# A hybrid DiT step on one core: triangular-solve lanes moved in and out by VectorE's 32x32 transposes

## The chip, the cores and the metric

The kernel runs on one core of a Trainium2 chip. The metric is device time in microseconds (us) of one execution, the median of three runs. A profile of one further execution gives the trace. Engines are named as the profile names them: PE is TensorE's matrix products, PEld its weight loads, DVE is VectorE, ACT is ScalarE, POOL is GpSimd, SP issues the transfers.

## The reference

One layer of a hybrid backbone for two request groups, 2048 "sample" tokens and 128 "prompt" tokens, model width 1024. One input projection feeds four branches (gated DeltaNet, a gated spatial unit, multi-scale pooling, a Fourier mix); one output projection joins them. The change concerns the DeltaNet branch. In chunks of 64 tokens it inverts a unit lower-triangular 64x64 matrix per chunk, head and direction:

```python
A = jnp.where(strict, jnp.einsum("nbhid,nbhjd->nbhij", kb, kc) * decay_mat, 0.0)
Tinv = lax.linalg.triangular_solve(eye + A, jnp.broadcast_to(eye, A.shape), left_side=True, lower=True)
u = jnp.einsum("nbhij,nbhje->nbhie", Tinv, vc * bc[..., None])
w = jnp.einsum("nbhij,nbhjd->nbhid", Tinv, kb * jnp.exp(gcum)[..., None])
...
(S_fin, o) = lax.scan(step, S0, (q_dec, k_dec, u, w, qk, g_last))
```

## The kernel before

Tokens come in three groups (`phase_a(gi)`: 768, 768 and 640 tokens, that is 12, 12 and 10 chunks). A group takes its normalized tokens (`x_fin`, line 334: transposes of x on PE into PSUM, evicted by ACT, split into a high and a low part by DVE and POOL), projects them with `mm3` (line 250: three fp32r products for each k, by far the most PE work), convolves, and prepares the recurrence of two head pairs (`pair_pre`). `pair_pre` multiplies keys with keys (line 673) and queries with keys (line 703) on PE, scales them by decays that come back from DRAM as broadcast rows (`Pd`, `Po`, `Pf`), and writes the two diagonal 32x32 blocks of each 64x64 matrix into `Ld` and the off-diagonal block into `Lo`.

The diagonal blocks are inverted in "lanes": each (pair, direction, chunk) of a half-chunk is one partition, the 32x32 matrix lies in the free dimension, and `lanes_solve` runs 30 steps of two DVE products over all lanes (lines 741 and 743). To get there, `lanes_in` transposes `Ld` on PE (line 731, 32 for a group) into the PSUM tag `pa`, and ACT evicts with a sign change into `LL` (line 734). To get back, `lanes_out` makes 128 products with an identity for each group (line 767), half of them after a DVE copy that reorders `LL` (line 762), evicted by ACT (lines 771, 775) and DVE (line 772) into `XF` and `XE`. Then the off-diagonal block follows from two products (lines 783 and 784, then 792 and 793), and the result goes to DRAM (`rec_d`), from where the scan (line 1053 on) reads it.

PSUM has four tags here: `pj` with 3 buffers (projections), `pa` with 2, `pb` with 2, `pc` with 1. A tag's buffers are handed out in the order in which the program asks for them. The order of instructions on each engine is made by a scheduler at build time, in which `lanes()` of one group is spread over the next group's projections. At run time each engine goes through its list in order, so an instruction that waits holds all behind it on its engine.

## Time and profile before

| | |
|---|---|
| median of 3 runs | 1212.36 us (1209.45 to 1213.25) |
| profiled execution, its own time | 1211.1 us |
| its span, first to last instruction | 1209.3 us |
| PE busy | 1090.1 us, 90% |
| DVE busy | 815.1 us, 67% |
| ACT, POOL busy | 417.9 us, 432.6 us |
| mean granted PE clock | 0.952 |

The span is 1.8 us under the profiled execution's own time. A share of busy time is an average over the whole span; what limits a stretch is read from the windows of that stretch. The stretch from 225 to 662 us holds all work on lanes of the three groups.

### The profile page before, as it was taken

To read this page: it belongs to the slowest core of one execution; us is meant where nothing else is said; L and a number is where in the kernel's file an instruction comes from. 1 tells how busy PE (TensorE), PEld (TensorE's weight loads), DVE (VectorE), ACT (ScalarE), POOL (GpSimd) and SP (SyncE) were. 2 spreads that over 40 slices of the span, in tenths; PEclk is the share of its full clock that TensorE was granted. 3 is DMA by queue.
4 is the path that set the end of the run, shared out by engine and by line. 5 is a ranking of instruction groups with operands and counts; after the bars stand their busy time and mean duration, and the time that the engine had idled before them with its cause. 6 is when DMAs were issued, how large, how long until landed. Compare 5 with 4: busy or idle time off the path is not lost.

```text
span 1209.3 us, 29864 instructions
## 1 busy us (share of the span) xinstructions
PE 1090.1 (90%) x12211; PEld 986.3 (82%) x12211; DVE 815.1 (67%) x1864; ACT 417.9 (35%) x837; POOL 432.6 (36%) x429
## 2 busy tenths in 40 slices
PE   5888988998799698898979989898999889999997
PEld 2488977998779697875879888887899778999997
DVE  3666886799974699934884633784243488878665
ACT  2355667656565756123123111121111211111211
POOL 1347364726442237510231242232135343433212
PEclk9899998999879799898999999999999989999999
DMA  9879549943644564645264556589355645544331
GB/s 309 302 250 316 139 120 232 279 131 83 148 114 104 126 151 112 192 142 143 70 187 125 160 165 211 181 262 306 89 160 167 213 136 166 173 133 150 106 131 70
DMA packets 251391, 204.28 MB, mean 169 GB/s; under 512 B 109138, under 2 KB 218706, under 8 KB 250998
## 3 DMA queue, kind: packets, MB, share of 16 engines
q1 hardware_dynamic: 251254, 202.37, 56.7%
q8 instruction: 96, 1.57, 0.5%
q14 instruction: 41, 0.34, 0.1%
HBM read 138.86 MB, written 63.46 MB: 167 GB/s over the span
## 4 chain that ended last, share of the span: by engine, by line
PE 45%; DVE 17%; DMA 11%; issue 4%; ACT 3%; SPq 1%; POOL 1%; DVEq 0%; ACTq 0%; POOLq 0%
PE pj L250 34%; PE pa L1053 3%; DMA wst<-in_wt_dram 2%; DVE LL L743 2%; DVE ltmp L741 2%; DVE BIG L243 2%; DVE acc L842 1%; DMA X<-xd_d 1%; DMA ada<-in_ada_dram 1%; PE pb L1295 1%; DMA hr<-h_d 1%; DMA wos<-in_wo_dram 1%; DVE BIG L240 1%; DMA wst<-in_wv_dram 1%; PE pb L1393 1%
## 5 line engine op out<-in xcount | busy, mean ns | idle before, releaser
L250 PE MATMUL pj<-BIG 128*128 128x256 f32 (+4 forms) x3888 | 615.9, 313 | 16.7 <-ACT g L1222 4.0
L250 PEld LDWEIGHTS pj<-BIG 128*128 128x128 f32 x3888 | 560.9, 195 | 36.2 <-issue 10.8
L250 PE MATMUL pj<-BIG,yh 128*128 128x256 f32 x1088 | 197.5, 286 | 3.6 <-ACT BIG L1355 2.4
L243 POOL TENSOR_TENSOR BIG<-wst,BIG 128x512 fp32r<-128x512 f32 (+1 forms) x66 | 96.0, 1455 | 235.4 <-DVE BIG L240 137.3
L250 PEld LDWEIGHTS pj<-BIG,yh 128*128 128x128 f32 x1088 | 164.6, 190 | 7.0 <-ACT BIG L1355 2.6
L250 PE MATMUL pj<-BIG,yl 128*128 128x256 f32 x544 | 141.3, 284 | 0.0
L250 PEld LDWEIGHTS pj<-BIG,yl 128*128 128x128 f32 x544 | 98.7, 190 | 0.7
L240 DVE CAST BIG<-wst 128x512 fp32r<-128x512 f32 (+2 forms) x72 | 38.6, 540 | 74.8 <-DMA wst<-in_wt_dram 34.5
L1060 POOL TENSOR_TENSOR gS<-S,sc_s 128x256 f32<-128x256 f32 x32 | 20.9, 655 | 133.8 <-DVE S L1075 128.3
L842 DVE SCALAR_TENSOR_TENSOR acc<-raw,prm,acc 128x768 f32<-128x768 f32 (+1 forms) x72 | 64.2, 908 | 5.5 <-ACT acc L840 5.5
L1374 ACT ACTIVATE yh<-yt 128x768 fp32r<-128x768 f32 (+1 forms) x34 | 20.7, 629 | 128.9 <-issue 47.3
L1222 ACT ACTIVATE g<-pj 128x256 f32<-128x256 f32 (+1 forms) x64 | 23.3, 396 | 118.3 <-PE pj L250 111.8
L243 DVE TENSOR_TENSOR BIG<-wst,BIG 128x512 fp32r<-128x512 f32 (+1 forms) x66 | 53.4, 808 | 15.9 <-ACT BIG L242 13.8
L1413 POOL TENSOR_TENSOR z<-z,xs 128x1024 f32<-128x1024 f32 x16 | 41.8, 2612 | 57.1 <-DVE z L1405 52.0
L741 DVE TENSOR_TENSOR ltmp<-LL 128x60 f32<-128x60 f32 (+14 forms) x90 | 53.6, 595 | 4.5 <-ACT LL L734 3.1
L743 DVE TENSOR_TENSOR LL<-LL,ltmp 128x60 f32<-128x60 f32 (+14 forms) x90 | 55.3, 614 | 1.4
L242 ACT ACTIVATE BIG<-wst 128x512 fp32r<-128x512 f32 (+1 forms) x60 | 37.6, 632 | 35.3 <-DMA wst<-in_wt_dram 14.0
L354 POOL TENSOR_TENSOR BIG<-h,BIG 128x384 fp32r<-128x384 f32 (+2 forms) x28 | 26.7, 953 | 54.0 <-DVE BIG L353 37.4
L1075 DVE TENSOR_TENSOR S<-pa,gS 128x256 f32<-128x256 f32 x34 | 14.3, 420 | 42.1 <-PE pc L1053 35.0
L1375 DVE TENSOR_TENSOR yl<-yt,yh 128x768 fp32r<-128x768 f32 (+1 forms) x34 | 37.3, 1112 | 7.8 <-ACT yh L1374 7.8
L1405 DVE TENSOR_TENSOR z<-pj,gbc 128x256 f32<-128x256 f32 x68 | 26.0, 419 | 22.5 <-PE pj L250 22.2
L1071 ACT ACTIVATE xn<-pa 128x256 f32<-128x256 f32 x34 | 12.9, 381 | 80.8 <-PE pa L1053 73.2
(291 smaller groups left out, 1846.1 us busy)
## 6 DMA issues: line engine op xcount, KB each, us to landing
wst<-in_wt_dram SPq DMA_DIRECT2D x96, 256.0 KB, 3.5
R<-rec_d SPq DMA_DIRECT2D x136, 128.0 KB, 3.1
ada<-in_ada_dram SPq DMA_DIRECT2D x24, 512.0 KB, 5.3
C<-com_d SPq DMA_DIRECT2D x68, 128.0 KB, 3.1
xs<-xs_d SPq DMA_DIRECT2D x16, 512.0 KB
out_dram<-z SPq DMA_DIRECT2D x16, 512.0 KB, 3.1
x<-in_xs_dram SPq DMA_DIRECT2D x13, 512.0 KB
xs_d<-x SPq DMA_DIRECT2D x13, 512.0 KB, 6.1
```

The lines of the kernel that those rows point to most:

```text
L240: nc.vector.tensor_copy(hi[:, ks, a:a + w], st[:, :, :w])
L242: nc.scalar.activation(hi[:, ks, a:a + w], st[:, :, :w], AF.Copy)
L243: (nc.vector if k0 == 0 else nc.gpsimd).tensor_tensor(lo[:, ks, a:a + w], st[:, :, :w], hi[:, ks, a:a + w].bitcast(F32), op=ALU.subtract)
L250: nc.tensor.matmul(out, lh[a](k), rh[b](k), start=(k == first and i == 0), stop=(k == last and i == 2))
L354: (nc.gpsimd if f % 2 else nc.vector).tensor_tensor(hT[1][:, f, off:off + w], h, hi.bitcast(F32), op=ALU.subtract)
L741: nc.vector.tensor_tensor(tv, X[:, :, j, j + 1:32].unsqueeze(2).to_broadcast([128, 2, j, ni]), bc(X[:, :, 0:j, j], ni), op=ALU.mult)
L743: nc.vector.tensor_tensor(X[:, :, 0:j, j + 1:32], X[:, :, 0:j, j + 1:32], tv, op=ALU.add)
L842: nc.vector.scalar_tensor_tensor(o, raw[:, si + j:si + j + n], w[:, j:j + 1], o, op0=ALU.mult, op1=ALU.add)
L1053: nc.tensor.matmul(ps[o, q], lh(q)[hp], rh[hp, q])
L1375: nc.vector.tensor_tensor(yl[:, q], yt[:, q], yh[:, q].bitcast(F32), op=ALU.subtract)
L1405: nc.vector.tensor_tensor(z[:, ns], ps, gbc[:, cd, ns], op=ALU.mult)
L1413: nc.gpsimd.tensor_tensor(z, z, xs, op=ALU.add)
```

## The change

`Ld` is laid out as [128, direction, 32 lanes, 32], and `lanes_in` becomes one DVE transpose of 32x32 blocks for each direction, from `Ld` straight into `LL`; a lane's partition now stands for one diagonal block of one pair and chunk, and the direction lies in the free dimension, where before the partition stood for pair, direction and chunk, and the two blocks lay in the free dimension. The solve's instructions keep their number and sizes. The sign goes into the factor `nb`, the negative of `be`. `lanes_out` becomes four DVE transposes for each group: two out of `LL` into new tiles `XT0`, `XT1`, two in place on `LL`. The products for the off-diagonal block read these directly; ACT copies the diagonal blocks into `XF` (8 copies of 32 partitions for each group), whose empty halves POOL clears first (2 memsets for each group, `lanes_tile`). `LL` has one buffer where it had two. The key and query products of `pair_pre` take their PSUM from `pa` (2 buffers) where they took it from `pb` (2 buffers). `x_fin` in `phase_a` alternates between `pc` and `pa` where it used `pc` alone.

```diff
+        nc.vector.tensor_scalar(g.nb, g.be, -1.0, None, op0=ALU.mult)
...
-        Ldv = Ld[:, :g.nu].rearrange("p (r d c) j -> p r d c j", r=2, d=2)
+        Ldv = Ld[:, :, pair * nch:(pair + 1) * nch]
...
-            ps = pb()
+            ps = pa()
...
-                nc.vector.tensor_tensor(Ldv[:, pair, d, cs], Pd[:, d, cs], psk[h2][:, 0], op=ALU.mult)
-            nc.gpsimd.tensor_tensor(Ldv[:, pair, d], Ldv[:, pair, d], bc(g.be[:, pair, d], 32), op=ALU.mult)
+                nc.vector.tensor_tensor(Ldv[:, d, cs], Pd[:, d, cs], psk[h2][:, 0], op=ALU.mult)
+            nc.gpsimd.tensor_tensor(Ldv[:, d], Ldv[:, d], bc(g.nb[:, pair, d], 32), op=ALU.mult)
...
-    def lanes_in(Ld, LL, jbs=range(8)):
-        for jb in jbs:
-            ps = pa()
-            for j in range(4):
-                nc.tensor.transpose(ps[:64, j * 128:j * 128 + 128], Ld[:, :, jb * 4 + j], ident)
-            pv = ps[:64].rearrange("p (j c b i) -> p j c b i", c=2, b=2, i=32)
-            for c2, cp in enumerate(HALF):
-                nc.scalar.activation(LL[cp, jb * 4:jb * 4 + 4], pv[:, :, c2], AF.Copy, scale=-1.0)
+    def lanes_in(Ld, LL, d):
+        nc.vector.transpose(LL[:, d], Ld[:, d].rearrange("p l j -> p j l"))
 
     def lanes_solve(LL, js=(1, 31)):
-        X = LL.rearrange("p c b i -> p b c i")
+        X = LL
...
-        dg = LL.rearrange("p c b i -> p (c b i)")
-        for b in range(2):
-            nc.gpsimd.memset(dg[:, b * 32:b * 32 + 31 * 65 + 1:65], 1.0)
-
-    def lanes_out(g, LL, Lo):
-        nch, nu = g.nch, g.nu
-        XF = ln_.tile([128, 3072], F32, tag="L6", name="XF", bufs=1)
-        XA = XF.rearrange("p (r x) -> p r x", r=2)[:, :, :2 * nch * 64].rearrange("p r (d c j) -> p r d c j", d=2, j=64)
+        dg = LL.rearrange("p d c i -> p d (c i)")
+        for d in range(2):
+            nc.gpsimd.memset(dg[:, d, 0:31 * 33 + 1:33], 1.0)
+
+    def lanes_tile(g):
+        t = ln_.tile([128, 3072], F32, tag="L6", name="XF", bufs=1)
+        XA = t.rearrange("p (r x) -> p r x", r=2)[:, :, :2 * g.nch * 64].rearrange("p r (d c j) -> p r d c j", d=2, j=64)
+        for d in range(2):
+            nc.gpsimd.memset(XA[:, :, d, :, 32 * d:32 * d + 32], 0.0)
+        return XA
+
+    def lanes_out(g, LL, Lo, XA):
+        nch = g.nch
         XF = [XA[:, r] for r in range(2)]
-        XE = ln_.tile([128, 2, NCC, 32], F32, tag="XE", name="XE", bufs=1)[:, :, :nch]
-        for d in (1, 0):
-            for b8 in range(4):
-                ps = pa()
-                X2 = LL[:, b8 * 8:b8 * 8 + 8]
-                if d == 0:
-                    X2 = ln_.tile([128, 8, 2, 32], F32, tag="X2", name="X2", bufs=2)
-                    nc.vector.tensor_copy(X2, LL[:, :, :, b8 * 8:b8 * 8 + 8].rearrange("p c b i -> p i b c"))
-                X2 = X2.rearrange("p e b c -> p e (b c)")
-                for e in range(8):
-                    for c2, cp in enumerate(HALF):
-                        rows = slice(c2 * 64, c2 * 64 + nu)
-                        nc.tensor.matmul(ps[cp, e * nu:e * nu + nu], X2[rows, e], ident[rows, rows])
-                pv = ps[:, :8 * nu].rearrange("p (e r d c) -> p d r c e", e=8, r=2, d=2)
-                sl = slice(b8 * 8, b8 * 8 + 8)
-                s2 = slice(32 + b8 * 8, 40 + b8 * 8)
-                nc.scalar.activation(XA[:, :, d, :, sl], pv[:, d], AF.Copy, scale=K("ma"))
-                nc.vector.tensor_scalar(XA[:, :, d, :, s2], pv[:, d], K("mb"), None, op0=ALU.mult)
+        XD, XE = [None, None], [None, None]
+        for d, flip in ((1, 0), (0, 0), (0, 1), (1, 1)):
+            t = LL[:, d] if flip else ln_.tile([128, 32, 32], F32, tag=f"XT{d}", name="XT", bufs=1)
+            te = t.rearrange("p l e -> p e l")
+            nc.vector.transpose(te, te if flip else LL[:, d])
+            t = t[:, :2 * nch].rearrange("p (r c) e -> p r c e", r=2)
+            if flip == d:
+                XE[d] = t
+            else:
+                XD[d] = t
                 for c2 in range(2):
-                    q = slice(c2 * 64 + 32 * (1 - d), c2 * 64 + 32 * (1 - d) + 32)
-                    nc.scalar.activation(XE[q, :, :, sl], pv[q, 1 - d], AF.Copy)
-                yield 1
+                    for b in range(2):
+                        q = slice(c2 * 64 + b * 32, c2 * 64 + b * 32 + 32)
+                        nc.scalar.activation(XA[q, :, d, :, b * 32:b * 32 + 32], t[q], AF.Copy)
+            yield 1
         for r in range(2):
             ps = pa()
             for c in range(nch):
                 for h2 in range(2):
                     a = slice(h2 * 64, h2 * 64 + 32)
                     b = slice(h2 * 64 + 32, h2 * 64 + 64)
...
-                    nc.tensor.matmul(ps[a, c * 32:c * 32 + 32], Lo[b, r, c], XF[r][b, 0, c, 32:64])
-                    nc.tensor.matmul(ps[b, c * 32:c * 32 + 32], Lo[a, r, c], XF[r][a, 1, c, 0:32])
+                    nc.tensor.matmul(ps[a, c * 32:c * 32 + 32], Lo[b, r, c], XD[0][b, r, c])
+                    nc.tensor.matmul(ps[b, c * 32:c * 32 + 32], Lo[a, r, c], XD[1][a, r, c])
...
-                    nc.tensor.matmul(ps[a, c * 32:c * 32 + 32], XE[a, r, c], M1[a, c])
-                    nc.tensor.matmul(ps[b, c * 32:c * 32 + 32], XE[b, r, c], M1[b, c])
+                    nc.tensor.matmul(ps[a, c * 32:c * 32 + 32], XE[0][a, r, c], M1[a, c])
+                    nc.tensor.matmul(ps[b, c * 32:c * 32 + 32], XE[1][b, r, c], M1[b, c])
...
-            x_fin(preps.pop(0))
+            x_fin(preps.pop(0), range(KC), (pc, pa))
...
-                    LL = ln_.tile([128, 32, 2, 32], F32, tag="LL", name="LL", bufs=2)
-
                     def lanes():
-                        for jb in range(8):
-                            lanes_in(Ld, LL, (jb,))
+                        LL = ln_.tile([128, 2, 32, 32], F32, tag="LL", name="LL", bufs=1)
+                        for d in range(2):
+                            lanes_in(Ld, LL, d)
                             yield 1
                         lin.pop()
+                        XA = lanes_tile(g)
                         for a, b in zip(SPL, SPL[1:]):
                             lanes_solve(LL, (a, b))
                             yield 1
-                        yield from lanes_out(g, LL, Lo)
+                        yield from lanes_out(g, LL, Lo, XA)
```

On PE, before: the products out of lanes of the second group (line 767), which stand behind the key and query products of the third group's second pair (lines 673 and 703; 1295 is the gate row's product). The off-diagonal products follow them.

```order
L673 MATMUL pb<-sl 32x64 x40
L250 MATMUL pj<-BIG 128x320 x31
L703 MATMUL pb<-sl 64x64 x20
L250 MATMUL pj<-BIG 128x320 x103
L767 MATMUL pa<-cm,LL 64x48 x32
L250 MATMUL pj<-BIG 128x320 x21
L767 MATMUL pa<-cm,LL 64x48 x32
L250 MATMUL pj<-BIG 128x320 x21
L767 MATMUL pa<-cm,X_5251 64x48 x16
L767 MATMUL pa<-cm,X_5274 64x48 x16
L250 MATMUL pj<-BIG 128x320 x11
L1295 MATMUL pb<-ada_6755,csil 2x256 x4
```

After, at the same place: the end of the off-diagonal products of the second group (785 and 786, the former 792 and 793), and behind them the third group's key products (674) and query products (704), now in `pa`.

```order
L785 MATMUL pa<-M_5073,XT 32x32
L786 MATMUL pa<-M_5073,LL 32x32
L674 MATMUL pa<-sl 32x64 x20
L1288 MATMUL pb<-ada_6128,csil 2x256 x4
L250 MATMUL pj<-BIG 128x320 x11
L1288 MATMUL pb<-ada_6134,csil 2x256 x2
L674 MATMUL pa<-sl 32x64 x20
L704 MATMUL pa<-sl 64x64 x10
L1288 MATMUL pb<-ada_6134,csil 2x256 x2
L250 MATMUL pj<-BIG 128x256 x16
L704 MATMUL pa<-sl 64x64 x10
```

The products out of lanes are gone, and the third group's key and query products have moved from ahead of the second group's off-diagonal products to behind them.

On DVE, before: the end of the second group's solve, the reordering copies (762) and the evictions (772), with weight casts (240, 243) between.

```order
L743 TENSOR_TENSOR LL<-LL,ltmp 128x2x29x2
L741 TENSOR_TENSOR ltmp<-LL 128x60
L743 TENSOR_TENSOR LL<-LL,ltmp 128x2x30
L762 COPY X_5251<-LL 128x512
L762 COPY X_5274<-LL 128x512
L772 TENSOR_SCALAR XF<-pa,cm 128x2x12x8 x4
L240 CAST BIG<-wst 128x4x136
L243 TENSOR_TENSOR BIG<-wst,BIG 128x4x136
L762 COPY X_5297<-LL 128x512
L772 TENSOR_SCALAR XF<-pa,cm 128x2x12x8
L762 COPY X_5320<-LL 128x512
L772 TENSOR_SCALAR XF<-pa,cm 128x2x12x8
```

After, at the same place: the end of the solve, the four transposes (759), and the products that follow (779 and 791 are the former 786 and 798; 684 is the former 683).

```order
L736 TENSOR_TENSOR ltmp<-LL 128x60
L738 TENSOR_TENSOR LL<-LL,ltmp 128x2x30
L759 STREAM_TRANSPOSE XT<-LL 128x32x32 x2
L759 STREAM_TRANSPOSE LL<-LL 128x32x32 x2
L779 TENSOR_TENSOR M_4967<-pa,m1s_1830 128x384
L791 COPY XF<-pa 32x12x32 x2
L779 TENSOR_TENSOR M_5073<-pa,m1s_1830 128x384
L240 CAST BIG<-wst 128x4x136
L243 TENSOR_TENSOR BIG<-wst,BIG 128x4x136
L791 COPY XF<-pa 32x12x32
L684 TENSOR_TENSOR Ld<-Pd,pa 128x160 x2
```

The four transposes follow the solve with nothing between, and nothing on DVE waits for PE there until line 779.

On PE, before: the second group's x transposes for the third group (342), all in `pc`, among the key products (673) and query products (703) in `pb`.

```order
L342 MATMUL pc<-cm,x 128x128 x3
L250 MATMUL pj<-BIG 128x384
L250 MATMUL pj<-BIG 128x392 x15
L342 MATMUL pc<-cm,x 128x128 x3
L673 MATMUL pb<-sl 32x64 x48
L250 MATMUL pj<-BIG 128x272 x19
L342 MATMUL pc<-cm,x 128x128
L250 MATMUL pj<-BIG 128x272 x7
L703 MATMUL pb<-sl 64x64 x11
L342 MATMUL pc<-cm,x 128x128
```

After: the same x transposes, in `pa` and `pc`, directly behind the query products (704), which are in `pa` too.

```order
L704 MATMUL pa<-sl 64x64 x24
L250 MATMUL pj<-BIG 128x392 x17
L342 MATMUL pa<-cm,x 128x128 x3
L643 MATMUL pb<-cm,sl 128x128 x6
L342 MATMUL pa<-cm,x 128x128 x6
L342 MATMUL pc<-cm,x 128x128 x3
L250 MATMUL pj<-BIG 128x272 x3
L342 MATMUL pa<-cm,x 128x128 x3
L250 MATMUL pj<-BIG 128x272 x24
L342 MATMUL pc<-cm,x 128x128 x3
L342 MATMUL pa<-cm,x 128x128
```

The x transposes and the key and query products now share the two buffers of `pa`, and the transposes have moved behind the query products.

## Rows read from the trace of the kernel before

**Rows 1.** The page: PE's and DVE's busy time, and PE's granted clock.

```profile
PE 1090.1 (90%) x12211; PEld 986.3 (82%) x12211; DVE 815.1 (67%) x1864; ACT 417.9 (35%) x837; POOL 432.6 (36%) x429
PEclk9899998999879799898999999999999989999999
```

**Rows 2.** The page: the chain that ended last, share of the span by engine.

```profile
PE 45%; DVE 17%; DMA 11%; issue 4%; ACT 3%; SPq 1%; POOL 1%; DVEq 0%; ACTq 0%; POOLq 0%
```

**Rows 3.** Windows: start:end, us, busy PE, PEld, DVE, ACT, POOL, clock, DMA, GB/s.

```profile
225.00:260.00 35.00, 33.35 (x240) 31.05 (x239) 32.35 (x70) 18.46 (x42) 16.50 (x16) 1.00 0.70 213
260.00:295.00 35.00, 31.43 (x190) 30.30 (x189) 34.72 (x51) 22.42 (x36) 14.82 (x17) 1.00 0.42 107
295.00:330.00 35.00, 28.57 (x296) 26.85 (x297) 34.79 (x64) 17.47 (x30) 20.92 (x20) 0.85 0.52 123
330.00:350.00 20.00, 18.06 (x219) 15.03 (x218) 15.23 (x55) 13.48 (x33) 5.45 (x11) 0.78 0.67 162
445.00:505.00 60.00, 55.54 (x481) 53.40 (x482) 59.54 (x112) 26.40 (x45) 35.95 (x48) 0.97 0.60 150
505.00:530.00 25.00, 21.03 (x264) 19.23 (x263) 11.98 (x24) 8.01 (x22) 3.59 (x4) 0.80 0.45 149
225.00:662.00 437.00, 390.74 (x4548) 351.95 (x4546) 337.25 (x686) 198.99 (x422) 154.69 (x176) 0.93 0.51 137
```

**Rows 4.** Windows of line L731 alone (transposes into lanes), PE.

```profile
225.00:260.00 35.00, 6.41 (x32) 4.01 (x32) 1.00 0.70 213
395.00:445.00 50.00, 5.36 (x32) 3.53 (x32) 0.86 0.53 123
550.00:580.00 30.00, 4.78 (x32) 3.47 (x32) 0.95 0.41 106
```

**Rows 5.** Windows of line L767 alone (products out of lanes), PE.

```profile
330.00:350.00 20.00, 9.31 (x146) 7.96 (x147) 0.78 0.67 162
350.00:395.00 45.00, 6.39 (x116) 5.29 (x114) 0.91 0.38 92
505.00:550.00 45.00, 9.86 (x256) 9.36 (x256) 0.84 0.56 176
610.00:645.00 35.00, 8.64 (x256) 7.93 (x256) 0.95 0.51 160
```

**Rows 6.** Groups by line, PE: busy, mean ns, idle before and its releaser.

```profile
L767 PE MATMUL pa<-cm,LL 48*64 48x48 f32 (+1 forms) x384 | 18.4, 253 | 6.1 <-DVE LL L743 4.0 <-ACT XE L775 2.1
L767 PE MATMUL pa<-cm,X 48*64 48x48 f32 (+1 forms) x384 | 15.8, 237 | 0.3 <-ACT XE L775 0.3
```

**Rows 7.** Groups by line, DVE: the lane copies and evictions; the weight casts.

```profile
L762 DVE COPY X<-LL 128x512 f32<-128x512 f32 x12 | 9.6, 824 | 0.1
L772 DVE TENSOR_SCALAR XF<-pa,cm 128x192 f32<-128x192 f32 (+1 forms) x24 | 9.7, 403 | 17.9 <-ACT XF L771 17.7
L240 DVE CAST BIG<-wst 128x512 fp32r<-128x512 f32 (+2 forms) x72 | 38.6, 540 | 74.8 <-DMA wst<-in_wt_dram 34.5 <-PE pj L250 32.6 <-DMA wst<-in_wv_dram 3.0
```

**Rows 8.** Groups by line, ACT: evictions into and out of lanes.

```profile
L734 ACT ACTIVATE LL<-pa 64x256 f32<-64x256 f32 x48 | 18.0, 375 | 25.8 <-PE pa L731 25.4
L771 ACT ACTIVATE XF<-pa,cm 128x192 f32<-128x192 f32 (+1 forms) x24 | 9.9, 411 | 27.5 <-PE pa L767 27.2
L775 ACT ACTIVATE XE<-pa 32x192 f32<-32x192 f32 (+1 forms) x48 | 15.0, 312 | 16.3 <-DVE XF L772 15.9
```

**Rows 9.** Timeline: DVE's solve beside a POOL product; start, us, what.

```profile
505.27 0.39 DVE L741 TENSOR_TENSOR ltmp<-LL 128x216 f32<-128x216 f32 x1
505.32 3.38 POOL L1244 TENSOR_TENSOR rw<-rw,g 128x640 f32<-128x640 f32 x2 [0.37 <-DMA rw<-raw_d]
505.69 1.61 DVE L743 TENSOR_TENSOR LL<-LL,ltmp 128x216 f32<-128x216 f32 x1
```

**Rows 10.** Waits: who for whom, total us, times, longest.

```profile
POOL Pf L692 <- DMA Pf<-pf_d: 16.3, 3, 10.6
```

**Rows 11.** Groups by form, POOL: the clearing of Ld.

```profile
L964 POOL MEMSET Ld<- 128x768 f32 x1 | 0.7, 742 | 3.6 <-PE pa L731 3.6
```

More of the change, by code (lines that the diff above doesn't have):

```diff
@@ L915, in phase_a @@
         if gi:
-            x_fin(preps.pop(0))
+            x_fin(preps.pop(0), range(KC), (pc, pa))
         if gi == 1:
-            x_fin(preps.pop(0))
+            x_fin(preps.pop(0), range(KC), (pc, pa))
         elif gi == 2:
-            x_fin(preps.pop(0))
-            x_fin(x_prep([(16, 128)], 512, None))
+            x_fin(preps.pop(0), range(KC), (pc, pa))
+            x_fin(x_prep([(16, 128)], 512, None), range(KC), (pc, pa))
         lg = sm_.tile([128, 6, 16], F32, tag="lg", name="lg", bufs=1)
```

8 lines of the change are left out of this document (4 added, 4 removed).

## Prediction

> **What bounds the kernel now.** I read the page first. PE is busy for 1090.1 of 1209.3 us, 90%, and its granted clock is near full in most slices [rows 1]; the chain that ended last runs through PE for 45% and through DVE for 17% [rows 2]. So the kernel is bound by PE, with stretches in which DVE is the later engine. An average doesn't say where, so I cut the stretch that holds the lanes, 225 to 662 us, into windows [rows 3]. Over the whole stretch PE is busy for 390.74 of 437 us and DVE for 337.25. The reader is to see that DVE has no room in three windows, 260 to 295, 295 to 330 and 445 to 505 us (34.72, 34.79 and 59.54 us busy of 35, 35 and 60): there PE time taken out comes back as PE idle time. In 330 to 350 and 505 to 530 us it is the other way round: DVE has 5 and 13 us of room, and PE works at a granted clock of 0.78 and 0.80. Then I read the lines that go, by window and by group.
>
> **What the change removes.** On PE, the 96 transposes of line 731 take 6.41, 5.36 and 4.78 us in the three groups [rows 4], together 16.55. The products of line 767 take 9.31 + 6.39 us in the first group, 9.86 in the second and 8.64 in the third [rows 5], together 34.20. That is 50.75 us of PE time; nothing of it moves to PE elsewhere. PE also stood idle for 6.1 + 0.3 = 6.4 us just before line 767 [rows 6]. On DVE, the copies of line 762 and the evictions of line 772 go, 9.6 + 9.7 = 19.3 us [rows 7]. On ACT, 18.0 + 9.9 + 15.0 = 42.9 us go [rows 8].
>
> **What it adds.** Six 32x32 transposes for each group on DVE, each of 128x1024, 18 in all. No row shows one. The nearest from below is the cast of line 240, 0.540 us for 512 elements, so 1.08 for 1024; from above the reordering copy of line 762, 0.824 us for 512 as a mean, so 1.65 [rows 7]. I take 1.3, in the lower half, because the transpose reads one tensor that it streams once, as the cast does, while the copy's mean holds some that were held up. 18 x 1.3 = 23.4 us (19.4 to 29.7), 4 us more than DVE loses. DVE's total thus hardly changes, and where it is full it stays full.
>
> On ACT come 24 copies of 32x768 (32x640 in the third group). Line 775 moves 192 elements in 0.312 us [rows 8]; four times that, 1.25 us, bounds one from above and 0.312 from below, so 7 to 30 us against the 42.9 removed. ACT is busy for 199 of 437 us in the stretch [rows 3], and the copies feed only the transfer to DRAM and not the next product, so I count them at nothing; without that cover the last group's copies would delay the scan's first load by 8 x 1.25 = 10 us at most. POOL gets six memsets of 128x768; one such took 0.742 us [rows 11], 4.5 us in all, issued ahead of the solve that separates them from their reader, and the solve covers them. The three multiplications for `nb` touch 48 elements for each partition, below the 216-element product's 0.39 us [rows 9]: 1.2 us at most, hidden while DVE has room.
>
> The Trainium skill, page "VectorE: DVE Perf Modes", section "The three transpose paths", speaks against my 1.3 us. It gives 311 ns for a 128x128 transpose on VectorE in a 16-bit type, and 390 ns on TensorE. Scaled to 1024 columns, an estimate from that page, a transpose here would take 2.49 us, 18 would take 44.8, and the sum below would end at 1183 in place of 1172. No row here shows a DVE transpose.
>
> **Where it lies on the path.** In the first group line 731's 6.41 us stand at the head of the full DVE stretch (DVE 32.35 of 35, then 34.72 of 35), so I count them at nothing. The other 44.34 us stand where PE limits or is the one waited for. The 6.4 us of idle time before line 767 go with it, but a new wait takes its place: the off-diagonal products now need three of the four outgoing transposes behind the solve, 3 x 1.3 = 3.9 us for each group, 11.7 in all (9.7 to 14.9), if no projection stands ahead of them on PE. Queued behind the waiting product are the next projections of line 250, so this counts in full. The incoming pair of transposes (2.6 us) replaces a passage through PE and ACT whose waits were 25.4 us at ACT [rows 8]; I count no gain for that.
>
> The sum: 50.75 - 6.41 + 6.4 - 11.7 = 39.0 us. From the profiled execution's 1211.1 us this gives 1172.1. The median of the runs is 1212.36, 1.3 us above that execution, so I forecast 1173.
>
> The tags. The key and query products exchange two buffers of `pb` for two of `pa`; in `pb` they shared with the transposes of tokens, in `pa` with the off-diagonal products and half the x transposes. In the third group the key products move behind the second group's off-diagonal products, since `pa` is handed out in order; the evictions that they then wait for are one for each engine (about 0.5 us), and projections stand between the two halves. I count the exchange at nothing; its price if that is wrong is the last rival. `LL` with one buffer makes the next group's incoming transposes wait for the last products that read it; in the trace of before the next group's line 731 runs from 395 us on, when the first group's work out of lanes (ended by 395) is over [rows 4, 5], so the wait is there already.
>
> **The rivals.**
>
> *DVE becomes the bound (1193 us).* All that is taken from PE before 505 us only brings PE sooner to where the second group's solve ends, and the full window 445 to 505 us decides that end. For it: 59.54 of 60 us busy; against it: between 330 and 350 us DVE has room and PE is busy for 18.06 of 20, so DVE's work there can come sooner with PE's. Lost are 6.41 + 9.31 + 6.39 + 5.36 = 27.47 us; 23.3 + 6.4 - 11.7 = 18.0 remain.
>
> *More comes back (1146 to 1154 us).* All 50.75 and the 6.4 count and projections cover the new waits: 1211.1 - 57.2 = 1154. If the idle time that goes also lifts the granted clock in 295 to 350 and 505 to 530 us (0.85, 0.78, 0.80), up to 0.15 x 28.57 + 0.22 x 18.06 + 0.20 x 21.03 = 12.5 us more are there; with two thirds of it 1146.
>
> *The transposes are slow (1183 to 1210 us).* At twice the upper bound, 3.3 us, the five of each group that stand on the chain (two in, three out) cost 49.5 us and the gain is gone. From about 2.5 us they cost 10 us more than I count. Against it: the copy of line 762 reorders with a stride too, and even its mean gives 1.65.
>
> A rule beside it concerns POOL. In the trace a solve product of 216 elements took 1.61 us while POOL multiplied, its neighbour of the same size 0.39 [rows 9]. The Trainium skill, page "SBUF — State Buffer", section "Who interferes with whom", says that a DVE instruction with two SBUF inputs is blocked by a POOL instruction that reads SBUF, and one with a single input outside the two-port modes is not; the trace agrees with the first half. By it a transpose would be spared such holds.
>
> *A wait on `pa` takes the place (slower, 1236 us).* The x transposes stand directly behind the query products in `pa`, and a query product's buffer is free only when `Pf` has come back from DRAM and passed POOL, ACT and DVE. POOL waited for that load for up to 10.6 us [rows 10]. If PE stands still that long behind each of the six pairs, 64 us are lost: 1173 + 63 = 1236. It decides from 39 / 6 = 6.5 us for each pair. Against it: `pb` was bound to the same chain before, and the key products now stand earlier in the first group.
>
> **How the numbers follow.** Chances: the forecast 0.52, DVE as the bound 0.18, more comes back 0.14, slow transposes 0.07 (0.03 of it without a measurable change), the wait on `pa` 0.09. The forecast's own range is 1158 to 1186 (the transposes' bounds and the order's changes). The range 1147 to 1200 takes in the second and most of the third and fourth case, and leaves out some 0.17. Within 0.3%, 3.6 us, a measurement of this kernel can't tell a change from none. Faster: 0.52 + 0.18 + 0.14 + 0.04 = 0.88; same 0.03; slower 0.09.
>
> **What would show it.** Right: PE busy near 1039 us, no PE row of lines 731 and 767, a transpose of 128x1024 near 1.3 us, DVE's busy time near 820 us, PE waiting for a transpose before the off-diagonal products for about 4 us a group, and the stretch of lanes shorter by some 39 us with the rest as long as before. Wrong: a transpose over 2.5 us; PE's idle time in the stretch (46 us before) grown by over 20 us and put down to DVE's solve; or PE waiting in `pa` behind `Pf`.

## The result, and the profile after

The changed kernel takes 1199.39 us (median of 4 runs, 1196.99 to 1202.51); the kernel before, beside it, 1212.32 us. The ratio is 0.9896 (95% interval 0.9861 to 0.9931): 12.6 us faster, where 39 were forecast. The time lies at the upper end of the range, and 26 us above the forecast. The profiled execution took 1200.81 us, its span is 1199.0 us.

The page of the changed kernel answers to [rows 1, 2]: PE's busy time, its granted clock by slice, and the chain that ended last.

```profile
PE 1058.8 (88%) x11347; PEld 958.3 (80%) x11347; DVE 842.1 (70%) x1849; ACT 401.8 (34%) x746; POOL 437.4 (36%) x435
PEclk9899896999879989989789999899999889999999
PE 40%; DVE 24%; DMA 11%; issue 5%; ACT 4%; SPq 2%; POOL 1%; DVEq 0%; ACTq 0%; POOLq 0%
```

PE is busy 31.3 us less, not 50.75; DVE 27 us more, not 4; DVE's share of the chain rose from 17% to 24%. Of DVE's 27 us, 16.0 are the transposes less what they replace (35.3, the sum of their groups below, less 19.3). Another 14.6 lie behind 840 us, at a subtraction that the change doesn't touch (line 1375 before, 1368 after):

```profile
L1375 DVE TENSOR_TENSOR yl<-yt,yh 128x768 fp32r<-128x768 f32 (+1 forms) x34 | 37.3, 1112 | 7.8 <-ACT yh L1374 7.8
L1368 DVE TENSOR_TENSOR yl<-yt,yh 128x768 fp32r<-128x768 f32 (+1 forms) x34 | 51.9, 1543 | 12.5 <-ACT yh L1367 12.5
```

The windows answer to [rows 3]:

```profile
225.00:260.00 35.00, 29.19 (x205) 27.48 (x205) 33.72 (x71) 14.91 (x28) 17.38 (x18) 1.00 0.61 197
260.00:295.00 35.00, 32.09 (x273) 30.26 (x272) 32.67 (x56) 22.06 (x34) 14.45 (x12) 1.00 0.45 111
295.00:330.00 35.00, 27.25 (x196) 24.56 (x195) 34.79 (x63) 21.67 (x34) 20.77 (x23) 0.87 0.53 125
330.00:350.00 20.00, 13.08 (x101) 12.09 (x100) 20.00 (x34) 14.55 (x24) 10.52 (x11) 0.84 0.67 183
505.00:530.00 25.00, 17.09 (x470) 10.19 (x468) 12.81 (x17) 9.53 (x15) 0.00 (x0) 0.80 0.50 145
225.00:662.00 437.00, 371.80 (x3909) 332.56 (x3908) 367.20 (x701) 185.86 (x340) 165.25 (x185) 0.92 0.54 147
```

In 330 to 350 us, where PE was busy for 18.06 of 20 us and DVE had room, DVE is now full and PE busy for 13.08. The clock in 505 to 530 us is still 0.80, though the products out of lanes that ran there are gone; the second group's off-diagonal products, among others, run there now (from 511 us on). The groups by line show the new instructions (busy, mean ns of one, idle before):

```profile
L729 DVE STREAM_TRANSPOSE LL<-Ld 128x1024 f32<-128x1024 f32 x6 | 12.2, 2042 | 0.0
L759 DVE STREAM_TRANSPOSE LL<-LL 128x1024 f32<-128x1024 f32 x6 | 12.0, 2052 | 0.0
L759 DVE STREAM_TRANSPOSE XT<-LL 128x1024 f32<-128x1024 f32 x6 | 11.1, 1927 | 0.2
```

A transpose takes 1.93 to 2.05 us as a mean of its group, 35.3 us in all. And the waits of PE in 225 to 662 us (who for whom, total us, times, longest):

```profile
PE pb L643 <- DVE qeps L594: 5.8, 3, 2.8
PE pa L776 <- DVE LL L759: 4.9, 1, 4.9
...
PE pb L588 <- DVE S L847: 4.1, 2, 3.6
PE pc L342 <- DVE x L331: 3.4, 2, 2.7
```

PE waited once for an outgoing transpose (line 776, first group, 4.9 us). Its other waits for DVE in these rows are at lines of which the change touches only the PSUM tag of line 342. Summed by the engine waited for, over 220 to 660 us:

| PE waited for, us | before | changed | e1 | e16 | e21 |
|---|---|---|---|---|---|
| DVE | 18.1 | 36.6 | 54.8 | 51.5 | 33.4 |
| ACT | 22.1 | 17.6 | 15.0 | 19.3 | 17.9 |

The idle time of the stretch grew by 19 us, and PE's waits for DVE grew by 18.5 (e1, e16 and e21 are experiments, described below).

**An account of the span.** For each window of 20 us I multiplied PE's busy time by the granted clock. The sum is PE's work at full clock; the rest of the busy time is lost to the lower clock; span less busy time is idle. The three make up the span. They are those of one profiled execution for each kernel, which lies up to 11 us from the median of its runs (e3: 1206.4 against 1195.3). With the steps of the clock as the trace has them, in place of windows, work is 1040.2 us before and 995.2 in the changed kernel; a term is good to some 4 us. The profiled execution of e18 took 3271.67 us, so e18 has no account.

| kernel | time, us | ratio to before (95%) | work | clock loss | idle |
|---|---|---|---|---|---|
| before | 1212.3 | | 1041.3 | 48.8 | 119.2 |
| changed | 1199.4 | 0.9896 (0.9861 to 0.9931) | 997.9 | 60.9 | 140.2 |
| e1 lanes only | 1221.6 | 1.0092 (1.0077 to 1.0107) | 994.0 | 71.5 | 154.8 |
| e2 tags only | 1237.9 | 1.0242 (1.0190 to 1.0293) | 1041.3 | 67.0 | 125.5 |
| e3 x in pc | 1195.3 | 0.9886 (0.9852 to 0.9920) | 1003.2 | 60.0 | 141.3 |
| e4 keys in pb | 1202.0 | 0.9925 (0.9897 to 0.9953) | 997.7 | 56.0 | 141.6 |
| e6 out, one eighth | 1184.9 | 0.9759 (0.9706 to 0.9811) | 1019.4 | 48.3 | 114.0 |
| e14 in, one quarter | 1229.8 | 1.0134 (1.0088 to 1.0181) | 1033.5 | 74.7 | 121.0 |
| e7 transposes twice | 1214.9 | 1.0005 (0.9973 to 1.0038) | 999.4 | 60.9 | 147.8 |
| e15 no flips | 1188.5 | 0.9799 (0.9746 to 0.9853) | 998.7 | 50.4 | 134.8 |
| e11 contiguous | 1203.0 | 0.9936 (0.9899 to 0.9973) | 1001.9 | 58.4 | 138.7 |
| e8 half of casts on ACT | 1195.1 | 0.9853 (0.9798 to 0.9909) | 996.7 | 49.8 | 144.6 |
| e12 = e11 and e8 | 1202.3 | 0.9889 (0.9855 to 0.9923) | 1000.2 | 51.6 | 140.0 |
| e18 all casts on ACT | 1198.5 | 0.9866 (0.9780 to 0.9953) | | | |
| e9 before, casts as e8 | 1219.7 | 1.0049 (1.0013 to 1.0086) | 1033.9 | 55.7 | 125.1 |
| e16 one step | 1220.5 | 1.0075 (1.0038 to 1.0111) | 996.6 | 58.4 | 163.0 |
| e17 tags swapped | 1196.0 | 0.9862 (0.9785 to 0.9939) | 997.4 | 60.8 | 143.3 |
| e19 more steps | 1202.1 | 0.9877 (0.9827 to 0.9928) | 1004.5 | 55.7 | 141.8 |
| e21 lanes only, later | 1208.0 | 0.9955 (0.9923 to 0.9987) | 997.9 | 68.1 | 136.2 |

The changed kernel has 43.4 us less work, 12.1 more clock loss and 21.0 more idle time: -10.3 us of span. Of the idle time 19.0 us (46.2 to 65.2) came in 220 to 660 us. The work column moves little among kernels with the same PE instructions (994 to 1005; before and e2 1041.3, but e9 1033.9), so a difference of 7 us in it says nothing; the other two columns decide. Differences in us below are ratios times 1212.3.

### The profile page after: what moved, and what is told of

Read it like the earlier page. It is cut to its first block, busy times and chain, and to the rows that moved or that the text cites. A ratio compares the mean times of both kernels' runs of the same rounds, so it can differ in the third digit from the quotient of the medians.

```text
span 1199.0 us, 28014 instructions
## 1 busy us (share of the span) xinstructions
PE 1058.8 (88%) x11347; PEld 958.3 (80%) x11347; DVE 842.1 (70%) x1849; ACT 401.8 (34%) x746; POOL 437.4 (36%) x435
## 4 chain that ended last, share of the span: by engine, by line
PE 40%; DVE 24%; DMA 11%; issue 5%; ACT 4%; SPq 2%; POOL 1%; DVEq 0%; ACTq 0%; POOLq 0%
PE pj L250 31%; DMA wst<-in_wt_dram 4%; PE pa L1046 3%; DVE acc L835 2%; DVE ltmp L736 2%; DVE LL L738 2%; DVE BIG L243 2%; DMA R<-rec_d 1%; DVE yl L1368 1%; PE pb L1288 1%; DVE BIG L1210 1%; POOL BIG L243 1%; DVE LL L729 1%; DVE BIG L240 1%; DMA ada<-in_ada_dram 1%
## 5 line engine op out<-in xcount | busy, mean ns | idle before, releaser
L250 PE MATMUL pj<-BIG 128*128 128x256 f32 (+4 forms) x3888 | 622.6, 317 | 23.9 <-ACT raw L816 6.0
L250 PEld LDWEIGHTS pj<-BIG 128*128 128x128 f32 x3888 | 571.9, 199 | 45.8 <-issue 11.2
L243 POOL TENSOR_TENSOR BIG<-wst,BIG 128x512 fp32r<-128x512 f32 (+1 forms) x66 | 99.9, 1513 | 210.6 <-DVE BIG L240 116.4
L250 PE MATMUL pj<-BIG,yl 128*128 128x256 f32 x544 | 138.0, 283 | 0.0
L835 DVE SCALAR_TENSOR_TENSOR acc<-raw,prm,acc 128x768 f32<-128x768 f32 (+2 forms) x72 | 66.4, 941 | 3.7 <-ACT acc L833 3.7
L243 DVE TENSOR_TENSOR BIG<-wst,BIG 128x512 fp32r<-128x512 f32 (+1 forms) x66 | 55.9, 847 | 16.4 <-ACT BIG L242 14.3
L1406 POOL TENSOR_TENSOR z<-z,xs 128x1024 f32<-128x1024 f32 x16 | 38.3, 2393 | 72.0 <-DVE z L1398 66.5
L1368 DVE TENSOR_TENSOR yl<-yt,yh 128x768 fp32r<-128x768 f32 (+1 forms) x34 | 51.9, 1543 | 12.5 <-ACT yh L1367 12.5
L736 DVE TENSOR_TENSOR ltmp<-LL 128x60 f32<-128x60 f32 (+14 forms) x90 | 55.7, 619 | 1.3
L354 POOL TENSOR_TENSOR BIG<-h,BIG 128x384 fp32r<-128x384 f32 (+2 forms) x28 | 28.9, 1031 | 57.5 <-DVE BIG L353 48.3
L353 DVE CAST BIG<-h 128x384 fp32r<-128x384 f32 (+2 forms) x56 | 27.1, 490 | 19.0 <-ACT h L344 19.0
```

The lines of the kernel that those rows point to most:

```text
L243: (nc.vector if k0 == 0 else nc.gpsimd).tensor_tensor(lo[:, ks, a:a + w], st[:, :, :w], hi[:, ks, a:a + w].bitcast(F32), op=ALU.subtract)
L250: nc.tensor.matmul(out, lh[a](k), rh[b](k), start=(k == first and i == 0), stop=(k == last and i == 2))
L353: nc.vector.tensor_copy(hi, h)
L354: (nc.gpsimd if f % 2 else nc.vector).tensor_tensor(hT[1][:, f, off:off + w], h, hi.bitcast(F32), op=ALU.subtract)
L736: nc.vector.tensor_tensor(tv, X[:, :, j, j + 1:32].unsqueeze(2).to_broadcast([128, 2, j, ni]), bc(X[:, :, 0:j, j], ni), op=ALU.mult)
L835: nc.vector.scalar_tensor_tensor(o, raw[:, si + j:si + j + n], w[:, j:j + 1], o, op0=ALU.mult, op1=ALU.add)
```

## The experiments

**Which part carries the gain (e1 to e4).** e1 is the changed kernel with the exchange of tags undone, e2 the kernel before with the exchange alone; e3 and e4 undo half of it in the changed kernel.

```diff
e1, e4, in pair_pre (twice):
-            ps = pa()
+            ps = pb()
e1, e3, in phase_a (four calls):
-            x_fin(preps.pop(0), range(KC), (pc, pa))
+            x_fin(preps.pop(0))
```

> The changed kernel with key and query products back in pb and x's transposes back in pc alone: only the lanes' transposes are new. If slow transposes on a full DVE took the missing gain (theory 1), it stays within 6 us of the changed kernel, 1193 to 1206 us. If the exchange of PSUM tags took it (theory 2), it lands near the forecast, 1170 to 1182 us. If the tags gave a part of the measured gain (theory 3), it is above 1206 us. PE busy near 1059 us in all three.

> The kernel before with key and query products in pa, which its lanes still use, and x's transposes on two tags: the other half of the change alone. Theory 1: within 6 us of before, 1206 to 1218 us. Theory 2: 15 to 25 us slower than before, 1227 to 1237 us. Theory 3: faster than before by 7 us or more. PE busy stays near 1090 us.

> The changed kernel with x's transposes in pc alone; key and query products stay in pa. Theory 2, if the waits on pa behind the query products are what costs: 10 to 25 us faster than the changed kernel, 1175 to 1190 us. Theory 1: within 6 us of it. Theory 3: up to 10 us slower.

> The changed kernel with key and query products back in pb; x's transposes stay on two tags. Theory 2, if the third group's key products behind the second group's off-diagonal products cost: 10 to 25 us faster than the changed kernel. Theory 1: within 6 us. Theory 3: up to 10 us slower, since the key products can no longer stand early beside the token transposes.

The lanes alone lose 11 us, the tags alone 29, and both together gain 12.6; either half of the exchange does as much as the whole. e1 is theory 3's case, e2 lies just above theory 2's range, so no theory holds for both; e3 and e4 stay within theory 1's 6 us. So the exchange that I counted at nothing is worth 24 us in the changed kernel (1.0092 to 0.9896). Why it costs 29 us in the kernel before stays open; the account has 18.2 us more of clock loss and 6.3 more of idle time for e2. The waits of PE in e1, 225 to 662 us:

```profile
PE pa L1046 <- DVE r L1058: 11.5, 2, 7.7
PE pb L1288 <- DMA ada<-in_ada_dram: 10.3, 4, 4.4
PE pc L342 <- DVE x L331: 7.9, 2, 5.4
PE pb L674 <- ACT tm L722: 6.4, 3, 4.1
PE pa L776 <- DVE LL L759: 6.4, 2, 4.2
...
PE pb L704 <- DVE Po L690: 4.0, 2, 2.3
```

Key and query products (lines 674 and 704) wait for 10.4 us; the longest waits are for data, not for PSUM (the scan's first steps at line 1046, a gate row's transfer at 1288).

**What a transpose costs (e5b).**

```diff
+            if not flip and d == 1 and g.gi == 2:
+                src = LL[:, 1]
+                fl, ft = src.rearrange("p c i -> p (c i)"), t.rearrange("p l e -> p (l e)")
+                nc.vector.transpose(ft, fl)
+                nc.vector.transpose(ft, fl)
+                nc.vector.transpose(t, src.rearrange("p c i -> p i c"))
+                nc.vector.transpose(te, src)
+                nc.vector.transpose(ft[:, 0:512], fl[:, 0:512])
+                nc.vector.transpose(ft[:, 0:128], fl[:, 0:128])
+                nc.vector.tensor_copy(ft, fl)
+                nc.vector.tensor_copy(te, src)
```

> The changed kernel with eight more VectorE instructions on scratch data ahead of the third group's first outgoing transpose, each on a source line of its own: transposes of 128x1024 with both sides contiguous (twice), with the source strided, with the destination strided, transposes of 512 and of 128 contiguous columns, and copies of 1024 elements with contiguous and with strided destination. It adds work and leaves nothing out. Theory A (a transpose costs about 2 ns an element whatever its strides): all four of 1024 near 2.0 us, 512 near 1.0, 128 near 0.26, the copies near 1.1. Theory B (the strided side costs): contiguous transposes near 1.1 us as the copies, strided ones near 2.0.

The groups by line; lines 762 to 769 are the eight calls in this order.

```profile
L765 DVE STREAM_TRANSPOSE XT<-LL 128x1024 f32<-128x1024 f32 x1 | 2.1, 2102 | 0.0
L764 DVE STREAM_TRANSPOSE XT<-LL 128x1024 f32<-128x1024 f32 x1 | 2.0, 1976 | 0.0
L768 DVE COPY XT<-LL 128x1024 f32<-128x1024 f32 x1 | 1.7, 1747 | 0.0
L762 DVE STREAM_TRANSPOSE XT<-LL 128x1024 f32<-128x1024 f32 x1 | 1.2, 1245 | 0.1
L763 DVE STREAM_TRANSPOSE XT<-LL 128x1024 f32<-128x1024 f32 x1 | 1.2, 1239 | 0.0
L769 DVE COPY XT<-LL 128x1024 f32<-128x1024 f32 x1 | 1.1, 1066 | 0.0
L766 DVE STREAM_TRANSPOSE XT<-LL 128x512 f32<-128x512 f32 x1 | 0.7, 714 | 0.0
```

The answer for line 767 alone (min/median/max ns, first and last start):

```profile
L767 DVE STREAM_TRANSPOSE XT<-LL x1: 298/298/298, 608.5 to 608.5; 128x128 f32<-128x128 f32 x1
```

Theory B: with both sides contiguous 1.24 us, with either side strided 1.98 to 2.10. From 128 to 1024 contiguous columns it grows by 944 ns, 1.05 ns a column. Each call ran once, and POOL multiplied beside the call with the strided destination (line 765) for 1.23 us; in the changed kernel the mean is 1.93 us with the destination strided and 2.04 with the source, so which side is strided makes no clear difference.

**What the removed PE work was worth (e6, e14).** Both are the kernel before with part of its lane products left out; the evictions read the products that remain several times.

```diff
e6, line 767 (one of eight products):
-                for e in range(8):
+                for e in range(1):
e14, line 731 (one of four transposes):
-            for j in range(4):
-                nc.tensor.transpose(ps[:64, j * 128:j * 128 + 128], Ld[:, :, jb * 4 + j], ident)
+            nc.tensor.transpose(ps[:64, :128], Ld[:, :, jb * 4], ident)
```

> The kernel before, in which line 767 makes one of its eight products for each tile and the evictions read that one eight times: seven eighths of the products out of lanes are left out, everything else stays, tags and order too. Theory A (the forecast's: a row's busy time is PE time that comes back where PE limits): 7/8 of 34.2 = 30 us less PE busy and most of 30 us less time, near 1183. Theory B (much of that busy time lies under other rows, and the waits on VectorE stay): PE busy less by 10 to 20 us, the time less by under 12 us.

> The kernel before, in which line 731 makes one of its four transposes for each tile and the evictions read that one four times: three quarters of the transposes into lanes are left out, 72 of 96, some 12.4 us by their rows. The rest stays. Theory A (a row's busy time comes back where PE limits; the first group's 4.8 us don't, VectorE being full): 6 to 10 us faster than before, near 1203. Theory B (all of it hidden, the passage is set by VectorE and by the evictions): within 3 us of before.

e6 gives 29 us back for rows of 7/8 x 34.20 = 29.9 us, the time of theory A. Its PE is busy only 22.4 us less (1090.1 to 1067.7), between the theories; 5.2 us more are idle time. Nor did the order stay: counted as in the table further below, its off-diagonal products stand behind 1230, 1886 and 2337 projections, before behind 1320, 1864 and 2274. So e6 doesn't show the worth of the rows alone.

e14 falls outside both theories: 72 transposes fewer, and 16 us slower. Its PE's idle time hardly changed (121.0 for 119.2); the loss is the clock (74.7 for 48.8), and it lies where PE is hardly idle. Two windows of the kernel before:

```profile
340.00:360.00 20.00, 19.91 (x244) 17.11 (x247) 15.52 (x37) 11.52 (x29) 10.08 (x10) 0.57 0.63 140
360.00:380.00 20.00, 20.00 (x259) 16.50 (x256) 8.70 (x24) 6.95 (x18) 5.87 (x8) 1.00 0.32 73
```

Windows of e14:

```profile
340.00:360.00 20.00, 18.01 (x225) 14.83 (x228) 14.34 (x42) 8.15 (x17) 9.14 (x13) 0.67 0.55 123
360.00:380.00 20.00, 20.00 (x148) 16.60 (x148) 6.18 (x15) 3.74 (x8) 3.74 (x5) 0.62 0.29 66
380.00:400.00 20.00, 20.00 (x130) 15.67 (x128) 7.91 (x20) 11.02 (x25) 4.25 (x6) 0.81 0.32 85
400.00:420.00 20.00, 20.00 (x158) 16.73 (x158) 7.54 (x20) 12.77 (x29) 2.81 (x5) 0.68 0.39 92
```

From 360 to 420 us PE is busy all the time, at a granted clock of 0.62 to 0.81, where before it had 1.00 in 360 to 380 us. In 340 to 420 us a projection took 402 ns as a mean, before 349, with the same number of key and query products between and about as many lane products; the 384 off-diagonal products that ran there before come later in e14. The order differs, since it is made at build time and a change of cost moves it everywhere. Why this order draws the lower clock is open.

**What VectorE's time costs (e7, e15, e11, e8, e12, e18, e9).** e7 issues 12 transposes twice; e15 leaves out the six in-place ones, so that lines 785 and 786 read blocks in the wrong orientation; e11 lays out `Ld` and `XT` so that 12 transposes are contiguous; e8 moves half of the casts to x's high part to ScalarE, e12 has both, e18 moves all casts, e9 is the kernel before with e8's move.

```diff
e7:
+        for _ in range(2):
             nc.vector.transpose(LL[:, d], Ld[:, d].rearrange("p l j -> p j l"))
...
+            for _ in range(1 if flip else 2):
                 nc.vector.transpose(te, te if flip else LL[:, d])
e15:
+            if not flip:
                 nc.vector.transpose(te, LL[:, d])
e11:
+        Ldv = Ld[:, :, :, pair * nch:(pair + 1) * nch].rearrange("p d j c -> p d c j")
...
+                nc.vector.transpose(t, LL[:, d])
+                t = t[:, :, :2 * nch].rearrange("p e (r c) -> p r c e", r=2)
e8, e9:
+        if late_x and f % 2 == 0:
+            nc.scalar.activation(hi, h, AF.Copy)
```

> The changed kernel with the two incoming transposes and the two into XT issued twice: 12 more transposes of about 2.0 us, 24 us more VectorE work, all of it on the chain from the lanes' input to the off-diagonal products. Theory A (transposes at 2.0 in place of 1.3 us account for what is missing of the gain: VectorE time in the lanes counts nearly in full): near 1220, 16 to 24 us above the changed kernel. Theory B (VectorE time there is mostly covered, the loss lies in order and tags): under 8 us more, below 1208.

> The changed kernel without the two in-place transposes of each group: 6 of 18 left out, 12.0 us of VectorE, and the products of lines 785 and 786 use blocks in the wrong orientation. Theory A (VectorE time in the lanes counts at about 0.65, as the doubled transposes did): 7 to 9 us faster than the changed kernel, near 1191. Theory B (only the transposes ahead of the first off-diagonal product count; of the flips one in each group stands there): 2 to 4 us, 1195 to 1197.

> The changed kernel with Ld laid out as direction, column, lane and XT as row, lane, so that the two incoming transposes and the two into XT have both sides contiguous; the in-place ones stay strided. The off-diagonal products then read XT with a stride of 32 elements. Theory A (a transpose with both sides contiguous takes 1.24 us as measured in the third group, and VectorE time in the lanes counts at 15.5 us for 24): 12 transposes at 0.75 us less are 9 us of VectorE and 5 to 6 us of time, near 1193. Theory B (strided writes of Ld on VectorE and GpSimd and strided reads of XT on PE take it back): within 3 us of the changed kernel, or slower, with lines 684, 685, 776 and 777 longer.

> The changed kernel with half of the casts to the high part of x (the even blocks in the three groups) moved from VectorE to ScalarE, some 12 of them in each group's stretch. Theory A (VectorE limits the stretches 225 to 345 and 445 to 505 us, so its relief there comes back): 4 to 10 us faster than the changed kernel, 1190 to 1196. Theory B (PE's waits are set by order and PSUM): within 3 us of the changed kernel.

> The one before, with half of the casts to the high part of x moved from VectorE to ScalarE as well. Theory A (VectorE's time counts at about 0.6 in the lanes' stretch): 9 + 12 us less of it, 10 to 13 us faster than the changed kernel, 1186 to 1190. Theory B (one of the two is enough, the rest is order): within 2 us of the better one alone, 1193 to 1195.

> The changed kernel with all casts to the high part of x in the groups' stretch moved from VectorE to ScalarE, twice the move of the half-casts run that stood at 1195. Theory A (VectorE's load sets PE's idle time and clock there): idle and clock loss together 8 to 14 us less than the changed kernel, near 1189. Theory B (order sets them): within 5 us of the changed kernel, either way, PE's busy time times clock unchanged at 998.

> The kernel before with half of the casts to the high part of x moved from VectorE to ScalarE. Theory A (VectorE's load is what the change made late; before it PE was the later engine): within 3 us of before. Theory B (VectorE's full windows limited the kernel before as well): 4 to 8 us faster, as in the changed kernel. Slower by more than 5 us would say that the order decides.

24 us more of transposes cost 13 us, between the theories of e7, and 12 us less give 12, more than either theory of e15: by these two, VectorE's time in the lanes counts for half or more. That is argued, since both also have another order (the third group's off-diagonal products stand behind 2232 and 2097 projections, in the changed kernel behind 2155), and e15's gain is 10.5 us of clock and 5.4 of idle time. And e11 saves some 9 us of transposes and is not faster (in its order PE waits for line 760's transposes 8.4 us, its writes of `Ld` take 9.4 us for 6.8, and its products that read the strided `XT`, lines 781 and 789, 18.5 us for 13.4), e12 is no better than e8 alone, and e8, e18 and the changed kernel can't be told apart. The same move makes the kernel before slower by 6 us (e9). Relief of VectorE alone doesn't decide.

**The order alone (e16, e17, e19, e21).** The work on lanes is handed out in steps (each `yield`) between projections. e16 merges steps, e17 begins the alternation of tags with the other one, e19 adds steps: the changed kernel's instructions, in another order. e21 is e1 with more steps.

```diff
e16, lanes_out and lanes():
-            yield 1
+        yield 1
...
-                            yield 1
+                        yield 1
e17:
-            x_fin(preps.pop(0), range(KC), (pc, pa))
+            x_fin(preps.pop(0), range(KC), (pa, pc))
e19, behind each outgoing transpose, and once more behind M1:
             yield 1
+            yield 1
e21 (on e1), behind each outgoing transpose:
             yield 1
+            yield 1
+            yield 1
+            yield 1
```

> The changed kernel in which the two incoming transposes are handed out as one step of the spread work and the four outgoing ones with the first off-diagonal products as one step: the same instructions in another order. Theory A (load, not order): within 3 us of the changed kernel. Theory B (order): 6 us or more away in either direction, with PE's busy time times clock at 998 and the difference in idle time and clock loss.

> The changed kernel in which the alternation of the x transposes in the three groups begins with the other tag (even blocks in pa, odd in pc): the same instructions and the same number of buffers in another order. Theory A (load, not order): within 3 us of the changed kernel. Theory B (order): 6 us or more away in either direction, all of it in idle time and clock loss.

> The lanes' part alone (key and query products in pb, x in pc alone), handed out with four steps behind each outgoing transpose in place of one. The off-diagonal products of the second and third group then stand behind 1848 and 2136 projections (1709 and 1961 in the lanes' part alone, 1824 and 2155 in the changed kernel); the first half of the first group's stays at 1128. Theory A (the place of these products behind the transposes set the loss): most of the 22 us comes back, 1198 to 1207. Theory B (the freed buffers of pa set it: keys and x wait for PSUM): it stays above 1214.

> The changed kernel with two steps behind each outgoing transpose and one more between the two passes of off-diagonal products: the same instructions, the second pass of the first group behind 1296 projections in place of 1261, those of the second group behind 1844 in place of 1824. Theory A (cover by projections is what the transposes lack): 3 to 8 us faster than the changed kernel, 1191 to 1196, by less idle time on PE. Theory B (the changed kernel has all the cover that counts): within 3 us.

e16 is 22 us slower than the changed kernel, with equal work and 23 us more idle time. What differs is the order. The number of projection products (line 250) that stand on PE ahead of the first off-diagonal product of each group is

| | first | second | third group |
|---|---|---|---|
| changed | 1240 | 1824 | 2155 |
| e3, e4, e17 | 1194, 1200, 1224 | 1824 each | 2157, 2126, 2155 |
| e19 | 1240 | 1844 | 2166 |
| e1 | 1128 | 1709 | 1961 |
| e16 | 1065 | 1792 | 2088 |
| e21 | 1128 | 1848 | 2136 |

The timeline of e16, DVE's outgoing transposes in the first group (start, us):

```profile
332.73 3.66 DVE L759 STREAM_TRANSPOSE XT<-LL 128x1024 f32<-128x1024 f32 x2
...
337.10 2.05 DVE L759 STREAM_TRANSPOSE LL<-LL 128x1024 f32<-128x1024 f32 x1
...
340.24 2.05 DVE L759 STREAM_TRANSPOSE LL<-LL 128x1024 f32<-128x1024 f32 x1
```

The timeline of e16, PE's first off-diagonal product, with the idle time before it:

```profile
342.44 0.23 PE L776 MATMUL pa<-LL,Lo 32*32 32x32 f32 x1 [8.78 <-DVE LL L759]
```

The windows of e16 around it:

```profile
320.00:340.00 20.00, 7.80 (x46) 5.88 (x46) 18.65 (x36) 10.97 (x16) 8.11 (x12) 0.50 0.79 191
340.00:360.00 20.00, 11.41 (x402) 9.58 (x403) 11.22 (x18) 13.06 (x19) 6.87 (x6) 0.50 0.45 109
```

PE reaches the off-diagonal products 175 projections earlier, stands 8.8 us behind the transposes with all later projections queued behind it, and the clock of the two windows is 0.50, the lower of PE's two levels. At line 776 PE waits for the transposes for 9.9 us in all, against 4.9 in the changed kernel; most of the 23 us lies in other waits (for DVE 14.9 us more in 220 to 660 us). It comes group by group: at the 1700th projection, by which both kernels have made as many other products (1703), e16's PE has been idle 9.8 us longer, at the 2000th, where that holds again (2271), 13.5, and at the end 22.8. That fewer projections ahead of the products that need DVE are the cause fits this and is argued; order changed elsewhere with it.

e21 pushes these products back in the lanes' part alone, with no freed buffer used: 16.6 of e1's 23.8 us come back, and idle time falls from 154.8 to 136.2, 4.0 us below the changed kernel's; what remains is clock loss, 68.1 for 60.9. It is theory A at its edge (1208.0; 1207 was its upper end). e17 and e19 stay within the changed kernel's interval: where the cover is there, more of it (e19) brings nothing. Nor is more of it a gain by itself: in e2 these products stand behind 1360, 1877 and 2396 projections, more than before, and e2 is slower.

## Why the prediction was wrong in size

**The removed work: right.** The rows hold 50.75 us of busy time at the clock granted in their windows [rows 4, 5]; times that clock they come to an estimated 45.1 us of work at full clock, and 43.4 us of work are gone (45.0 by the clock's own steps). PE's busy time fell by less, 31.3 us, because 12.1 us more are lost to the clock.

**The step that failed** is the sum, "50.75 - 6.41 + 6.4 - 11.7 = 39.0 us". It treats the removed rows' busy time as returned and one wait as the only price. For the lanes alone, which it prices, it failed by more than the result shows: e1, with the exchange of tags undone, took 1221.6 us where 1173 was forecast, outside the range. That the changed kernel lies inside it, by 0.6 us, is luck: the exchange, counted at nothing, gave 24 us. Two things were left out of the sum:

- *Idle time*: 11.7 us of new waits were set against 6.41 and 6.4; PE's idle time rose by 21.0. The wait that I named is small, 4.9 us in the first group and none in the others. The rest are waits for other DVE work that is late: line 643 for `qeps`, 588 for `S`, 342 for x; PE's waits for DVE doubled, from 18.1 to 36.6 us. That is the rival "DVE becomes the bound" in part. As it said, the second group's solve hardly moves: it ends at 505.4 us where it ended at 510.5, though 27.47 us of PE's rows are gone ahead of it. But the third group's solve ends 31 us earlier (588.1 for 619.0), and PE's waits aren't put down to the solve. The sign that I had set down, idle time in the stretch grown by over 20 us, is just missed (18.9, from 46.3 to 65.2). The sentence "DVE's total thus hardly changes" fell with the size of a transpose: 35.3 us against 23.4, 16.0 more than what went, where 4 were counted. 1.3 us was taken from a cast with contiguous sides, and here one side or both are strided. With 2.0 us the same sum would have given 39.0 - (18 - 11.7) = 32.7 us, so this size alone isn't it.
- *The clock*: I let it only rise ("More comes back"). It fell: 0.952 to 0.937 in the profiles, 0.933 to 0.940 in all four runs after, and 12.1 us more are lost to it. Most of the removed rows ran at 0.78 to 0.95 [rows 4, 5]; their slow stretches stayed slow, as 505 to 530 us shows. In the profile the growth lies in 0 to 220 us (12.0 to 18.9) and behind 660 us (8.7 to 14.2). At its 1000th projection the changed kernel is already 8.2 us late (300.0 us, before 291.8), having lost 8.0 us more to the clock by its own steps; most of the removed rows come behind that. One place of the growth is where the x transposes now follow each other with few projections between, and PE waits 2.48 and 1.98 us for ACT (window of the changed kernel):

```profile
180.00:200.00 20.00, 16.19 (x80) 12.85 (x81) 20.00 (x38) 15.38 (x24) 13.98 (x11) 0.52 0.83 231
```

Before, this window had 0.86. But e17 has 11.5 us of clock loss in 0 to 220 us and the same time, so I can't say that this place sets it.

**"I count the exchange at nothing": wrong by 24 us**, with the opposite sign to the rival that I priced. PE's waits in `pa` behind `Pf` don't show after: no wait of lines 674 and 704 is among them. e21 shows that order alone, with no buffer freed, brings back 16.6 of the 24 us, and e16 that order alone loses 22. How the exchange does it is read from the table and argued: the off-diagonal products take their buffers from the same tag, fall behind more projections, and these cover DVE's work. What the last 7 us between e21 and the changed kernel come from, buffers or the first group's half that stays at 1128, is open (the account has them as clock loss), as is the cause of the clock's fall outside the stretch.

**The transposes.** The trace has 298 ns for 128 contiguous columns (fp32) and 1.24 us for 1024. The Trainium skill, page "VectorE: DVE Perf Modes", section "The three transpose paths", has 311 ns for 128x128 in a 16-bit type, close to the first, and led to an estimate of 2.49 us for 1024: scaling by eight counts a fixed part eight times. That the estimate came nearer to the 2.04 of the strided transposes than 1.3 did is an accident. The 18 transposes took 1.88 to 2.17 us, the one at 232.2 us, beside POOL at work throughout, 2.13, where a product with two inputs went from 0.39 to 1.61 [rows 9]. By the Trainium skill, page "SBUF — State Buffer", section "Who interferes with whom", a transpose would be spared POOL's holds, and the trace agrees.

**Counted at nothing, and rightly:** the 24 ACT copies (0.81 us each, 19.4 in all, waited for by no row of PE), and `LL` with one buffer, as far as rows show it (no idle time before line 729); it wasn't undone by itself. The three multiplications for `nb` took 1.7 us, not 1.2 at most: one ran for 1.36 us, the others for 0.17 and 0.18.

None of the variants that do the whole work beats the changed kernel by more than the intervals allow; e8, e3 and e17 stand at 1195 to 1196.

## What to carry to other kernels

Split the span into PE work at full clock, time lost to the clock and idle time before pricing a removal: the first moves as the rows say, taken at the clock granted to them, the other two can take most of it back. Where the order is made at build time, ask for each instruction that waits on the slower engine how many independent products stand ahead of it, and compare the order with and without each part; a part that seems to free a buffer may act by order alone. An experiment that removes work gets another order too and can be slower (e14, by clock loss), so read it with its account, not by its time alone.
